# Reordering token loads, pooling chains and norms around a TensorE-bound decoder block

## The chip, the cores and the metric

The kernel runs on one NeuronCore of one Trainium2 chip, as one launch. The metric is the device time of that launch in microseconds (us). The core has five engines that run their own instruction streams in order: TensorE (PE: matmuls, with its weight loads shown apart as PEld), VectorE (DVE), ScalarE (ACT), GpSimd (POOL) and SyncE (SP, which only issues DMAs here). They meet through semaphores. On-chip memory is SBUF (128 partitions) and PSUM, eight banks of 128 x 512 f32 into which TensorE writes.

## The reference, cut to what matters

One hybrid decoder block over 512 tokens of 1024 channels, in f32:

```python
h = rms_norm(x, g_mix_pre)
z = h @ w_in                      # pool 512 | rnn x 1024 | rnn gate 1024 | merge gates 2 x 1024
y_pool = pool_mixer(z_pool) @ w_pool_out   # per group: trailing mean over 2, 4, 8, 16 tokens minus the token, then a 128 x 128 map
y_rnn = rg_lru(z_x, z_g) @ w_rg_out        # causal conv of 4, gates, linear recurrence over tokens, times gelu(z_g)
merged = sigmoid(z_a) * y_pool + sigmoid(z_b) * y_rnn
x = x + rms_norm(merged @ w_o, g_mix_post)
up = rms_norm(x, g_ffn_pre) @ w_up
x = x + rms_norm((gelu(conv3(up_a)) * up_b) @ w_down, g_ffn_post)
ple = rms_norm(p @ w_ple_proj, g_ple_post)
out = x + sigmoid(rms_norm(x, g_ple_gate) @ w_ple_gate) * ple
```

`rms_norm` divides each token by the root of its mean square over all 1024 channels, so each norm needs a sum over a whole token before anything behind it can start.

## The kernel before, in words

**Precision.** TensorE is fed with numbers of fewer bits than f32. Every operand is split into a high half, a rounded copy made by ScalarE (`ACT.copy` into an `fp32r` tile, shown as CAST), and a low half, the difference, made by VectorE (`sub`, line 189). A product then takes three matmuls (`mm3`, lines 219 to 221): high by high, high by low, low by high. So each weight tile needs a DMA (line 426), a ScalarE cast (line 433) and a VectorE subtraction before TensorE can use all of it.

**Weights.** `plan` lists every weight tile in the order of use, and `weight(key, ahead)` prepares up to `ahead` tiles (mostly 4) beyond the one wanted (`prep`). Raw, high and low tiles have six buffers each. Intermediate tiles of 128 x 512 (`slot`) come from a pool of 25 buffers, scratch (`temp`) from one of 5.

**Order of the work.** TensorE's instructions keep the order in which the program is written. Those of the other engines are placed by a planner: it walks through an estimate of the run, and gives each free engine the ready instruction of highest priority. The priority is the place in the program; `tc.high_priority(offset=n)` moves it up by n instructions, and `urgent()` by 700. `behind(ins, name)` fixes the order of two instructions on one engine. Once placed, the order is fixed, and at run time each engine takes its instructions strictly one after another.

**Stages**, in order of time:

1. *Start* (0 to 29 us). `x_t`, the tokens with channels on partitions, arrives in eight pieces of 256 KB; `ht(k)` is the piece times its gain, as high (line 487) and low half (line 488). Four column tiles of the rnn input are computed together from weight pieces rx 0 to rx 3 (line 524). The norm is not applied here: the tokens are loaded once more with tokens on partitions, in two DMAs of 1 MB (`xtok`, line 493), ScalarE squares and sums them (line 507, four instructions), GpSimd raises to the power -0.5 (`rsqrt`, line 455), and VectorE puts the four columns on diagonals (line 515), which TensorE spreads over the partitions with a matrix of ones (`spread_rstd`, line 569) inside the first input tile. The result `rb` is multiplied in when a tile is read from PSUM (`scaled`, line 583). DRAM-to-DRAM sums of weight blocks are issued by GpSimd from behind that `rsqrt` on (line 293).
2. *Input tiles* (29 to 99 us): tiles 0 to 11 of `w_in` (`in_tile`, 24 matmuls each), with conv and the small per-head gate matmuls between them. Then `rnn_decay` (lines 641 to 656, exponentials on ScalarE and scans on VectorE), `rnn_out` and `rnn_split`.
3. *Gate and pool tiles* (99 to about 205 us), in `IN_ORDER`: four gate tiles, then pool tile 0, gate 4, pool 1, gate 5, pool 2, gate 6, pool 3, gate 7, then map 0, gate 8, map 1 and so on. `pool_tile(g)` reads the tile out (`scaled` at offset 300), adds shifted copies log2(window) times (line 712), forms the difference from the token (lines 717 to 719) and splits it (`split`); `pool_map(g)` multiplies it with `pool_w`. `gate_tile` reads out at offset 300 too.
4. *Merge and output projection* (205 to 305 us), with `w_o` by a seven-product scheme on halves. At the end `x2_sum` and `x2_out` form the residual and its norm per token tile (`add_norm`, `rstd_of`), and `h2_tile` transposes and splits it.
5. *Embedding projection* (305 to 317 us): `ple_tile(t)` for four token tiles, all at offset 2100: two PSUM banks of products, each copied to SBUF (lines 769 and 770) and sent to DRAM; `rstd_of(pair)` squares the two banks (line 462). All squares of `rstd_of` are kept in program order by `last_square`.
6. *Up projection* (317 to 366 us for the first part) and *down projection* (to 659 us), again by the seven-product scheme.
7. *End* (650 to 710 us): `x3_norm(t, pair)` makes the second residual and its norm (`add_norm`: line 871 reads the sums, line 462 squares them, line 874 adds; line 1185 applies the gain), `x3_tile(t)` transposes (line 879) and splits it, and the loop from line 1253 on computes the gate in two column halves h with `wpg` weights, four token tiles each. The subtraction for the `wpg` weights of h = 0 has an offset of 1400 (line 434).

Of the kernel before, what the change touches and what calls it, by code (L numbers as in the profile page):

```python
# [14 lines left out]
P = 128  # L15
S = 512
# [65 lines left out]
def block_kernel(  # L82
# [53 lines left out]
    def quad(tag, dt=F32R, place=0):  # L136
        t = big.tile([P, 4 * S + PLACES], dt, tag=tag, name=nm(tag))
        return t[:, place : place + 4 * S].rearrange("p (a c) -> p a c", a=4)
# [23 lines left out]
    def act(o, i, func, after=None, **kw):  # L162

        ins = ACT.activation(o, i, func, **kw)  # L164
        after = after or last_func[0]
        if after is not None:
            behind(ins, after)
        last_func[0] = ins.ins.name
        return ins
# [18 lines left out]
    def sub(o, a, b):  # L188
        V.tensor_tensor(o, a, b, ALU.subtract)  # L189
# [49 lines left out]
    def c1(j):  # L239
        return col[:, j : j + 1]  # L240
# [162 lines left out]
    def prep(key):  # L403
        if key[0] == "up" and key not in parts:
            up_form(*key[1:])
            return
        if key in parts:
            hi, lo = parts_of(D)
            for i, v in enumerate((hi, lo)):
                nc.sync.dma_start(v.bitcast(F32), parts[key][i])  # L410
            if key[0] == "up":
                hi, lo = (v.rearrange("p (j c) -> p j c", j=2) for v in (hi, lo))
            ready[key] = (hi, lo)
            return
        ap = src[key]
        n = 1
        for d in ap.shape[1:]:
            n *= d
        raw = wpool.tile([P, n], F32, tag="raw", name=nm("raw"), bufs=6)
        dst = raw if len(ap.shape) == 2 else raw.rearrange("p (k c) -> p k c", k=ap.shape[1])  # L420
        if key == order[0]:
            nc.sync.dma_start(xraw[0], x_t[0])
            for a, b in FIRST:
                nc.sync.dma_start(raw[:, a:b], ap.rearrange("p k c -> p (k c)")[:, a:b])
        else:
            nc.sync.dma_start(dst, ap)
        hi, lo = parts_of(n)
        if key == order[0]:
            for a, b in FIRST:
                ACT.copy(hi[:, a:b], raw[:, a:b])  # L430
                sub(lo[:, a:b], raw[:, a:b], hi[:, a:b].bitcast(F32))
        else:
            ACT.copy(hi, raw)  # L433
            with tc.high_priority(offset=2 * URGENT if key[0] == "wpg" and key[2] == 0 else 300 if key[0] == "in" and key[1] >= 12 else 0):
                sub(lo, raw, hi.bitcast(F32))
        ready[key] = (hi, lo)

    def weight(key, ahead=AHEAD):
        i = order.index(key)
        while nxt[0] <= min(i + ahead, len(order) - 1):  # L440
            prep(order[nxt[0]])
            nxt[0] += 1
        return ready[key]
# [11 lines left out]
        last_pow[0] = nc.gpsimd.tensor_tensor(y, v, mhalf[:, :n], ALU.pow).ins.name  # L455
        return y

    def rstd_of(halves):
        sums = []
        for hsrc in halves:  # L460
            s = tiny()
            ins = ACT.activation(rb, hsrc, AF.Square, scale=1.0 / 32.0, accum_out=s)  # L462
            if last_square[0] is not None:
                behind(ins, last_square[0])
            last_square[0] = ins.ins.name
            sums.append(s)
        v = tiny()
        V.scalar_tensor_tensor(v, sums[0], EPS, sums[1], ALU.add, ALU.add)  # L468
        return rsqrt(v)
# [7 lines left out]

    xraw = [slot() for _ in range(KD)]
    xtok = []
    for k in range(KD):  # L480
        raw = xraw[k]
        if k == 0:
            weight(("rx", 0), ahead=0)
        else:
            nc.sync.dma_start(raw, x_t[k])
        hi, lo = ht(k)
        ht_done = ACT.activation(hi, raw, AF.Identity, scale=c1(C_GMIX + k)).ins.name
        V.scalar_tensor_tensor(lo, raw, c1(C_GMIX + k), hi.bitcast(F32), ALU.mult, ALU.subtract)
        if k % 2 == 1 and k < 7:
            if k > 1:  # L490
                xt = quad("C", F32)
                a = k // 2 - 1
                nc.sync.dma_start(
                    xt.rearrange("p (a h) c -> p a (h c)", a=2),
                    x[2 * a * P : 2 * (a + 1) * P, :].rearrange("(a p) c -> p a c", p=P),
                )
                xtok.append(xt)
            weight(("rx", k // 2 + 1), ahead=0)


    ssq = tiny(NT)
    for a in range(2):
        xt = xtok[a]
        for b in range(2):
            v = xt[:, 2 * b : 2 * b + 2, :]
            t = 2 * a + b
            ACT.activation(v, v, AF.Square, scale=1.0 / 32.0, accum_out=ssq[:, t : t + 1])
    v4 = tiny(NT)
    V.tensor_scalar(v4, ssq, EPS, None, ALU.add)
    rstd1 = rsqrt(v4, NT)  # L510
# [31 lines left out]
    sp = [const.tile([P, 8], F32, tag=f"sp{i}", name=f"sp{i}") for i in range(7)]  # L542
    mabs, e, f, s, s2, ncol, n2col = sp
    V.scalar_tensor_tensor(mabs, lam, -1.0, lam, ALU.mult, ALU.min)
    act(e, mabs, AF.Exp, after=ht_done)
    V.tensor_scalar(f, e, 1e-37, None, ALU.max)
    act(f, f, AF.Ln)
    sub(f, mabs, f)
# [24 lines left out]
    def in_tile(m):  # L573
        w = weight(("in", m), ahead=AHEAD if m > 6 else AHEAD0)
        ps = bank()
        for k in range(KD):
            mm3(ps, pick(w, k * P, (k + 1) * P), ht(k), k == 0, k == KD - 1)
            if m == 0 and k == 2:
                spread_rstd()
        return ps  # L580

    def scaled(ps, o):
        return V.tensor_tensor(row(o), back(ps), row(rb), ALU.mult)
# [115 lines left out]
    yp, pools = {}, {}  # L699

    def pool_tile(g):
        w = WINDOWS[g]
        ps = in_tile(12 + g)
        u = temp(n=S + PAD)
        V.memset(u[:, :PAD], 0.0)
        with tc.high_priority(offset=300):
            scaled(ps, u[:, PAD:])
        acc, d = u, 1
        while d < w:
            nx = temp(n=S + PAD)  # L710
            o = 2 * d if 2 * d < w else PAD
            V.tensor_tensor(nx[:, o:], acc[:, o:], acc[:, o - d : S + PAD - d], ALU.add)
            acc, d = nx, 2 * d
        u = u[:, PAD:]
        acc = acc[:, PAD:]
        dd = temp()
        V.scalar_tensor_tensor(dd[:, w - 1 :], acc[:, w - 1 :], 1.0 / w, u[:, w - 1 :], ALU.mult, ALU.subtract)
        V.tensor_tensor(acc[:, : w - 1], acc[:, : w - 1], col[:, C_RC : C_RC + w - 1], ALU.mult)
        sub(dd[:, : w - 1], acc[:, : w - 1], u[:, : w - 1])
        hi, lo = slot(F32R), slot(F32R)  # L720
        split(hi, lo, dd)
        pools[g] = hi, lo
# [36 lines left out]
    def ple_tile(t):  # L759
        pair = []  # L760
        for h in range(2):
            w = weight(("wpp", h))
            ps = bank()
            for k in range(2):
                a = pick(pq[k], t * P, (t + 1) * P)
                mm3(ps, a, pick(w, k * S, (k + 1) * S), k == 0, k == 1)
            pair.append(ps)
        outs = [slot(), slot()]
        V.tensor_copy(row(outs[0]), back(pair[0]))
        ACT.copy(row(outs[1]), back(pair[1]))  # L770
        s = rstd_of(pair)
        rp[t] = const.tile([P, 1], F32, tag=f"rp{t}", name=f"rp{t}")
        V.tensor_copy(rp[t], s)
        for h, o in enumerate(outs):
            nc.sync.dma_start(pled[t * P : (t + 1) * P, h * S : (h + 1) * S], o)


    def product(name, lhs, f, banks, start, head=0, tail=0):
# [259 lines left out]

    for t in range(NT):
        with tc.high_priority(offset=3 * URGENT):  # L1040
            ple_tile(t)
        if t == 0:
            x2_out(2)
            x2_sum(3, (oz[1], o5[:, 1]))
        if t == 1:
            h2_tile(1)
            x2_out(3)
    for kind, n in O_AFTER:
        if kind == "tr":
            h2_tile(n)  # L1050
        elif kind == "up":
            up_plain(n, 0)
        else:
            up_product(n, 1)
# [123 lines left out]

    def x3_norm(t, pair):
        res = [x3[t // 2][:, 2 * (t % 2) + h, :] for h in range(2)]  # L1180
        with tc.high_priority(offset=URGENT if t > 1 else 0):
            add_norm(pair, (gq[:, 0, :], gq[:, 1, :]), res)
            for h in range(2):
                x3n[t, h] = nq[t // 2][:, 2 * (t % 2) + h, :]
                V.tensor_tensor(x3n[t, h], res[h], gq[:, 2 + h, :], ALU.mult)
        s3 = rstd_of(res)
        r3[t] = const.tile([P, 1], F32, tag=f"r3{t}", name=f"r3{t}")
        V.tensor_copy(r3[t], s3)

    def x3_tile(t):  # L1190
        xq = hquad(F32R)
        for h in range(2):
            ps = transposed(x3n[t, h])
            x3t[t, h] = xq[:, 2 * h, :], xq[:, 2 * h + 1, :]
            with urgent():
                split(*x3t[t, h], ps)

    gq = quad("C", F32)
# [153 lines left out]
```

## Time and profile before

| | |
|---|---|
| median of 3 runs | 711.7 us (711.26 to 713.67) |
| profiled execution | 712.31 us, span 710.3 us |
| granted TensorE clock | 1.00 |
| TensorE matmul / weight load busy | 699.5 / 637.0 us |
| VectorE, ScalarE, GpSimd busy | 576.6, 441.0, 82.3 us |
| DMA | 172.53 MB, mean 243 GB/s |

The profile is one execution. Its page groups the instructions by line and engine with their busy time, mean length and the idle time before them; the waits name, for each engine, who released it. A timeline row reads: start, length, engine, line, operation, tiles written and read, shapes, count, and in brackets the idle time before it with its releaser. A row of the stretches reads: the stretch, its length, the busy time of TensorE, its weight loads, VectorE, ScalarE and GpSimd, each with its count, then the granted clock, the DMA share and GB/s. Matmuls overlap in the trace, so their lengths add up to more than the time they hold the engine.

### The profile page before, as it was taken

Reading aid. Unit: us, or ns where it says so; the run is one execution under the profiler, and the core shown is the slowest. Engines: PE = TensorE matmul, PEld = TensorE weight load, DVE = VectorE, ACT = ScalarE, POOL = GpSimd, SP = SyncE. Lnnn points to the kernel's source line nnn. Section 1 sums busy time; section 2 is a strip of 40 time slices with the busy share of each in tenths; the row PEclk is TensorE's granted clock in tenths of the full one; section 3 lists DMA queues with packets and bytes.
Section 4 is the critical chain, followed back from the end, with each engine's and each line's share of the span. In section 5 each row is a group of like instructions: output and inputs, shape, how many; then the busy total and the mean of one; then the engine's idle time right before and its main releaser. Section 6 shows DMA issues by size and latency. Waiting matters only on the chain.

```text
span 710.3 us, 11245 instructions
## 1 busy us (share of the span) xinstructions
PE 699.5 (98%) x4281; PEld 637.0 (90%) x4281; DVE 576.6 (81%) x749; ACT 441.0 (62%) x670; POOL 82.3 (12%) x107
## 2 busy tenths in 40 slices
PE   9999999999999999999999999999999999999897
PEld 7888888888888888889999999999999888888786
DVE  3897745999756578776989899899999999789852
ACT  6756789854643245487866677666667766574721
POOL 0311111110000000120013222222200000010100
PEclk9999999999999999999999999999999999999999
DMA  8999787765698999995379999999967677868011
GB/s 318 386 314 279 189 237 162 179 150 189 235 345 271 318 339 357 334 327 187 124 261 267 263 310 251 317 241 337 230 196 232 202 248 229 282 194 290 7 60 59
DMA packets 64933, 172.53 MB, mean 243 GB/s; under 512 B 5808, under 2 KB 6448, under 8 KB 64560
## 3 DMA queue, kind: packets, MB, share of 16 engines
q1 hardware_dynamic: 50336, 129.78, 52.7%
q0 software_dynamic: 14400, 41.95, 25.1%
q8 instruction: 33, 0.54, 0.3%
q14 instruction: 20, 0.16, 0.1%
q10 hardware_dynamic: 144, 0.10, 0.1%
HBM read 155.03 MB, written 58.72 MB: 301 GB/s over the span
## 4 chain that ended last, share of the span: by engine, by line
PE 75%; DVE 12%; ACT 5%; DMA 3%; issue 2%; POOL 1%; SPq 0%; DVEq 0%; POOLq 0%; ACTq 0%
PE ps L219 25%; PE ps L220 25%; PE ps L221 24%; DVE lo L189 3%; ACT m L164 1%; DMA C<-in_x_dram 1%; POOL s L455 1%; DVE m L656 1%; ACT t L164 1%; ACT rb L462 1%; DVE C L189 1%; DMA m<-in_x_t_dram 1%; DVE m L947 1%; PE ps L627 1%; DVE A L1258 1%
## 5 line engine op out<-in xcount | busy, mean ns | idle before, releaser
L189 DVE TENSOR_TENSOR lo<-raw,hi 128x1024 fp32r<-128x1024 f32 (+2 forms) x193 | 224.3, 1184 | 54.3 <-ACT hi L433 40.1
L219 PE MATMUL ps<-A,hi 128*128 128x256 f32 (+1 forms) x608 | 194.5, 320 | 0.0
L220 PE MATMUL ps<-A,hi 128*128 128x256 f32 (+1 forms) x608 | 193.8, 319 | 0.0
L221 PE MATMUL ps<-A,lo 128*128 128x256 f32 (+1 forms) x608 | 193.8, 319 | 0.0
L433 ACT CAST hi<-raw 128x1024 fp32r<-128x1024 f32 (+1 forms) x112 | 112.3, 1010 | 94.4 <-PE ps L220 28.3
L219 PEld LDWEIGHTS ps<-A,hi 128*128 128x128 f32 x608 | 115.9, 191 | 8.4 <-issue 1.3
L221 PEld LDWEIGHTS ps<-A,lo 128*128 128x128 f32 x608 | 116.0, 191 | 6.9
L220 PEld LDWEIGHTS ps<-A,hi 128*128 128x128 f32 x608 | 116.0, 191 | 6.7
L219 PE MATMUL ps<-C,hi 128*128 128x256 f32 (+1 forms) x392 | 114.7, 293 | 1.5 <-ACT rb L462 1.2
L220 PE MATMUL ps<-C,hi 128*128 128x256 f32 (+1 forms) x392 | 114.3, 291 | 0.0
L221 PE MATMUL ps<-C,lo 128*128 128x256 f32 (+1 forms) x392 | 114.3, 291 | 0.0
L193 ACT CAST hi<-raw 128x1024 fp32r<-128x1024 f32 x78 | 80.5, 1050 | 20.5 <-PE ps L220 12.2
L219 PE MATMUL ps<-hi,A 128*128 128x512 f32 x224 | 85.3, 381 | 0.0
L220 PE MATMUL ps<-lo,A 128*128 128x512 f32 x224 | 84.9, 379 | 0.0
L221 PE MATMUL ps<-hi,A 128*128 128x512 f32 x224 | 84.9, 379 | 0.0
L219 PEld LDWEIGHTS ps<-C,hi 128*128 128x128 f32 x392 | 74.7, 190 | 3.9 <-ACT rb L462 1.5
L220 PEld LDWEIGHTS ps<-C,hi 128*128 128x128 f32 x392 | 74.7, 191 | 1.8
L221 PEld LDWEIGHTS ps<-C,lo 128*128 128x128 f32 x392 | 74.7, 191 | 1.7
L455 POOL TENSOR_TENSOR s<-s,mhalf 128x1 f32<-128x1 f32 (+1 forms) x21 | 15.7, 749 | 343.0 <-DVE s L468 323.1
L219 PEld LDWEIGHTS ps<-hi,A 128*128 128x128 f32 x224 | 42.3, 189 | 6.3 <-ACT hi L433 0.3
L221 PEld LDWEIGHTS ps<-hi,A 128*128 128x128 f32 x224 | 42.3, 189 | 6.0
L220 PEld LDWEIGHTS ps<-lo,A 128*128 128x128 f32 x224 | 42.3, 189 | 5.9
(191 smaller groups left out, 1024.7 us busy)
## 6 DMA issues: line engine op xcount, KB each, us to landing
raw<-in_w_up_dram SPq DMA_DIRECT2D x46, 512.0 KB, 8.1
wdsum<-in_w_down_dram POOLq DMA_DIRECT2D x36, 512.0 KB, 9.1
raw<-in_w_in_dram SPq DMA_DIRECT2D x32, 512.0 KB, 7.1
raw<-wdsum SPq DMA_DIRECT2D x24, 512.0 KB, 4.2
raw<-in_w_down_dram SPq DMA_DIRECT2D x18, 512.0 KB, 4.4
wosum<-in_w_o_dram POOLq DMA_DIRECT2D x12, 512.0 KB, 9.7
wdsum<-wdsum POOLq DMA_DIRECT2D x12, 512.0 KB, 8.0
parts<-hi SPq DMA_DIRECT2D x10, 512.0 KB, 5.0
```

Source lines behind the costliest of these rows:

```text
L164: ins = ACT.activation(o, i, func, **kw)
L189: V.tensor_tensor(o, a, b, ALU.subtract)
L193: last_copy[0] = ACT.copy(hi, src)
L219: PE.matmul(o, ah, bh, start=start, stop=False, **kw)
L220: PE.matmul(o, ah, bl, start=False, stop=False, **kw)
L221: PE.matmul(o, al, bh, start=False, stop=stop, **kw)
L433: ACT.copy(hi, raw)
L455: last_pow[0] = nc.gpsimd.tensor_tensor(y, v, mhalf[:, :n], ALU.pow).ins.name
L462: ins = ACT.activation(rb, hsrc, AF.Square, scale=1.0 / 32.0, accum_out=s)
L627: PE.matmul(ps, bd[pr, a, o], turns(b[pr]), start=i == 0, stop=i == 2)
L656: V.tensor_tensor_scan(r, a_t[c], r, 0.0, ALU.mult, ALU.add)
L947: V.scalar_tensor_tensor(h2n[t, h], res[h], r, g_pre[h], ALU.mult, ALU.mult)
```

## The change

Four groups of edits.

- *Start.* The two token loads (`load_tokens`) are issued after rx 3 and after the last `x_t` piece; before, they stood ahead of rx 2 and ahead of rx 3. The square of token tile 0 is placed behind the activation of `x_t` piece 5, the other three behind that of piece 7.
- *Pool chains.* Everything of a pool tile behind its matmuls (`pool_mean`) runs under `urgent()`. The split of the first input tile's weights is urgent as well.
- *Embedding norms.* `ple_tile` only computes, copies and stores; `ple_norm` squares the SBUF copies, is called after the x2 steps of the same token tile, has no offset, and its squares leave the fixed order of squares.
- *Last norms.* `x3_norm` of token tiles 2 and 3 and the splits of their transposes get an offset of 2800; before, 700. The squares for the second norm of every token tile leave the fixed order.

```diff
@@ prep
+        elif key == ("in", 0):
+            with urgent():
+                split(hi, lo, raw)
@@ rstd_of
-    def rstd_of(halves):
+    def rstd_of(halves, in_order=True):
...
-            if last_square[0] is not None:
+            if in_order and last_square[0] is not None:
                 behind(ins, last_square[0])
-            last_square[0] = ins.ins.name
+            if in_order:
+                last_square[0] = ins.ins.name
@@ start
+    ht_done = []
+
+    def load_tokens(a):
+        xt = quad("C", F32)
+        nc.sync.dma_start(
+            xt.rearrange("p (a h) c -> p a (h c)", a=2),
+            x[2 * a * P : 2 * (a + 1) * P, :].rearrange("(a p) c -> p a c", p=P),
+        )
+        xtok.append(xt)
...
-        ht_done = ACT.activation(hi, raw, AF.Identity, scale=c1(C_GMIX + k)).ins.name
+        ht_done.append(ACT.activation(hi, raw, AF.Identity, scale=c1(C_GMIX + k)).ins.name)
...
         if k % 2 == 1 and k < 7:
-            if k > 1:
-                xt = quad("C", F32)
-                a = k // 2 - 1
-                nc.sync.dma_start(
-                    xt.rearrange("p (a h) c -> p a (h c)", a=2),
-                    x[2 * a * P : 2 * (a + 1) * P, :].rearrange("(a p) c -> p a c", p=P),
-                )
-                xtok.append(xt)
             weight(("rx", k // 2 + 1), ahead=0)
+        if k in (5, 7):
+            load_tokens(k // 2 - 2)
...
-            ACT.activation(v, v, AF.Square, scale=1.0 / 32.0, accum_out=ssq[:, t : t + 1])
+            behind(ACT.activation(v, v, AF.Square, scale=1.0 / 32.0, accum_out=ssq[:, t : t + 1]), ht_done[7 if t else 5])
...
-    act(e, mabs, AF.Exp, after=ht_done)
+    act(e, mabs, AF.Exp, after=ht_done[-1])
@@ pool_tile
     def pool_tile(g):
+        ps = in_tile(12 + g)
+        with urgent():
+            pool_mean(g, ps)
+
+    def pool_mean(g, ps):
         w = WINDOWS[g]
-        ps = in_tile(12 + g)
         u = temp(n=S + PAD)
         V.memset(u[:, :PAD], 0.0)
-        with tc.high_priority(offset=300):
-            scaled(ps, u[:, PAD:])
+        scaled(ps, u[:, PAD:])
@@ ple_tile
-        s = rstd_of(pair)
+        for h, o in enumerate(outs):
+            nc.sync.dma_start(pled[t * P : (t + 1) * P, h * S : (h + 1) * S], o)
+        return outs
+
+    def ple_norm(t, outs):
+        s = rstd_of(outs, in_order=False)
         rp[t] = const.tile([P, 1], F32, tag=f"rp{t}", name=f"rp{t}")
         V.tensor_copy(rp[t], s)
-        for h, o in enumerate(outs):
-            nc.sync.dma_start(pled[t * P : (t + 1) * P, h * S : (h + 1) * S], o)
@@ embedding loop
         with tc.high_priority(offset=3 * URGENT):
-            ple_tile(t)
+            outs = ple_tile(t)
         if t == 0:
             x2_out(2)
             x2_sum(3, (oz[1], o5[:, 1]))
         if t == 1:
             h2_tile(1)
             x2_out(3)
+        ple_norm(t, outs)
@@ x3_norm
-        with tc.high_priority(offset=URGENT if t > 1 else 0):
+        with tc.high_priority(offset=4 * URGENT if t > 1 else 0):
             add_norm(pair, (gq[:, 0, :], gq[:, 1, :]), res)
...
-        s3 = rstd_of(res)
+        s3 = rstd_of(res, in_order=False)
@@ x3_tile
-            with urgent():
+            with tc.high_priority(offset=(4 if t > 1 else 1) * URGENT):
                 split(*x3t[t, h], ps)
```

## The prediction

> **What bounds the kernel now.** I read the page first, then the waits of TensorE's weight loads, then the timeline around each of those waits.
>
> ```profile
> span 710.3 us, 11245 instructions
> PE 699.5 (98%) x4281; PEld 637.0 (90%) x4281; DVE 576.6 (81%) x749; ACT 441.0 (62%) x670; POOL 82.3 (12%) x107
> ```
>
> TensorE is busy for 699.5 of 710.3 us, so only the time in which it waits can be won. The waits of its weight loads (engine, line, releaser: us in total, times, longest):
>
> ```profile
> PEld ps L879 <- DVE h L1185: 2.1, 1, 2.1
> ...
> PEld ps L219 <- ACT rb L462: 1.5, 1, 1.5
> PEld ps L220 <- DVE m L189: 1.3, 1, 1.3
> PEld ps L524 <- DVE lo L189: 1.1, 1, 1.1
> PEld ps L524 <- ACT A L487: 1.0, 2, 0.6
> PEld ps L219 <- ACT m L905: 0.6, 1, 0.6
> PEld ps L221 <- DVE h L189: 0.5, 1, 0.5
> ```
>
> Each of the four parts of the change stands at one or two of these rows. Those in its reach: 2.1 + 1.5 + 1.3 + 1.1 + 0.6 (the longer L487 wait) + 0.6 + 0.5 = 7.7 us. That is the most that it can win.
>
> The Trainium skill ("Perfetto Trace Analysis", section "Identifying the Most-Contended Engine") holds matmul busy time a bad measure and takes the busy share of the weight loads. By that share, 90% in the row above, 73 us would be free instead of 7.7, an estimate by that page. The trace does not agree: a load lasts 637.0 / 4281 = 0.15 us on average, while a matmul of 512 columns holds the chain of work for 0.22 us (row below) where nothing waits, so the loads' idle share is no waiting and no end of my range comes from it.
>
> ```profile
> 29.14 0.22 PE ps L220
> ```
>
> **Part A: token loads and squares later.** ScalarE, then the end of the rstd chain that the first input tile needs:
>
> ```profile
> 13.55 1.06 ACT L507 ACTIVATE C<-C 128x1024 f32<-128x1024 f32 x1 [1.62 <-DMA C<-in_x_dram]
> ...
> 16.58 1.33 ACT L487 ACTIVATE A<-m,col 128x512 fp32r<-128x512 f32 x2
> ...
> 18.74 1.06 ACT L507 ACTIVATE C<-C 128x1024 f32<-128x1024 f32 x1 [0.83 <-DMA C<-in_x_dram]
> ...
> 20.84 1.03 ACT L433 CAST hi<-raw 128x1024 fp32r<-128x1024 f32 x1
> ...
> 22.28 0.88 DVE L515 TENSOR_SCALAR t<-ident,s 128x128 f32<-128x128 f32 x4 [1.15 <-POOL s L455]
> ...
> 24.15 1.28 ACT L164 ACT_TABLE_LOAD   x1
> ...
> 30.50 1.07 PEld L569 LDWEIGHTS ps<-t,m 128*128 128x128 f32 x8
> ```
>
> ScalarE waits 1.62 us, then 0.83 us, for the token DMAs, with casts and activations that TensorE wants queued behind. The four squares themselves (about 1.05 us each) stand ahead of the activations at 16.58 and the cast at 20.84. TensorE then waits for the activation (0.6) and the low half of that cast (1.1). Two DMAs of 1 MB move: the first from before rx 2 to after rx 3, the second from before rx 3 to behind x 6 and x 7. No instruction is added. On SP's queue, rx 2, x 4, x 5 and rx 3 each pass 1 MB, and rx 3 passes the second MB too. From 13.55 to 18.74, 2 MB landed (rx 2, x 4, x 5, second token load): 0.39 MB per us. So rx 3 should land at 13.55 - 2.6 + 3.9 = 14.9 against TensorE's need at about 22; the last token load behind 1 MB more, at 18.74 + 2.6 = 21.3. The gain is 0.6 + 1.1 = 1.7; counted at matmul starts, which a load wait shifts by less, about 1.4. I take 1.3; bounds 0 and 1.7.
>
> What is late next: rstd. Two squares after 21.3 end at 23.4 instead of 20.84, so the diagonals end at 23.16 + 2.6 = 25.8. TensorE wants them at 30.50 - 1.4 = 29.1: 3.3 us of cover. The first input tile's cast and low half, now urgent, add 1.03 us to ScalarE's queue there, inside that cover. The POOL queue's DRAM sums, issued behind the rsqrt, start 2.6 us later; that queue idles 137 us later on (row in part C), so nothing waits for them.
>
> The Trainium skill ("ScalarE: Activation LUTs", section "Table sets: the hidden batching unit") says functions come in table sets and only cheap fillers are in each. Squares that fall behind the logarithm's load could need another. With two loads (the page's 2.66 us each, an estimate by it) the cover of 3.3 us would be gone by 2.0. No run here shows squares under that set.
>
> **Part B: pool chains urgent.** VectorE and ScalarE, and the stretch:
>
> ```profile
> 128.60 0.67 DVE L583 TENSOR_TENSOR t<-ps,rb 128x512 f32<-128x512 f32 x1
> ...
> 144.51 2.36 DVE L189 TENSOR_TENSOR lo<-raw,hi 128x1024 fp32r<-128x1024 f32 x2
> ...
> 154.60 0.69 DVE L712 TENSOR_TENSOR t<-t 128x512 f32<-128x512 f32 x1
> ...
> 159.66 0.62 ACT L193 CAST m<-t 128x512 fp32r<-128x512 f32 x1 [6.62 <-DVE t L189]
> ...
> 161.29 0.69 DVE L189 TENSOR_TENSOR m<-t,m 128x512 fp32r<-128x512 f32 x1
> ...
> 161.90 0.69 DVE L583 TENSOR_TENSOR m<-ps,rb 128x512 f32<-128x512 f32 x1
> ...
> 126.00:162.00 36.00, 35.12 (x163) 30.42 (x161) 35.84 (x59) 23.08 (x36) 5.87 (x7) 1.00 0.68 165
> ```
>
> Group 0's sum is read out at 128.60 but its one add waits until 154.60, behind the whole recurrence; its low half ends at 161.98 and TensorE has waited 1.3 us (L220 <- DVE m). With the chain at 700 instead of 300 for its first step and 0 for the rest, group 0 needs a sum, an add, a difference and a low half, 4 x 0.69 plus two corrections of some 0.15: 3.1 us, done near 132. The wait goes: 1.2 taken, bounds 1.3 and a loss below. VectorE is full here (35.84 of 36.00), so the work is traded: groups 0 to 2 (1, 2, 3 adds) take 3.1 + 3.8 + 4.5 = 11.4 us, of which group 0's 3.1 ran there already; up to 8.3 us of recurrence, high/low splits and gates go behind. The splits are wanted only after eight more gate tiles, 40 us on. The nearest cover is that of the weights' low halves: the first of the pair at 144.51 ends by 145.7, and its tile starts two tiles of 24 x 0.22 = 5.3 us before the wait near 161, at 150.5: 4.8 us. These keep an offset of 300 against 0 for the recurrence, so they should stay ahead of it.
>
> **Part C: embedding norms from the copies.** POOL's wait, the squares, and the copies:
>
> ```profile
> 293.38 0.57 POOL L455 TENSOR_TENSOR s<-s,mhalf 128x1 f32<-128x1 f32 x1 [137.34 <-DVE s L468]
> ...
> 317.06 0.60 ACT L462 ACTIVATE rb<-ps 128x512 f32<-128x512 f32 x1
> ...
> 319.41 0.66 ACT L462 ACTIVATE rb<-m 128x512 f32<-128x512 f32 x1
> ...
> 321.76 1.42 DVE L947 SCALAR_TENSOR_TENSOR m<-m,s,m 128x512 f32<-128x512 f32 x2 [0.66 <-POOL s L455]
> ...
> 323.09 1.28 DVE L769 COPY m<-ps 128x512 f32<-128x512 f32 x2
> ...
> 323.89 0.60 ACT L462 ACTIVATE rb<-ps 128x512 f32<-128x512 f32 x1 [2.02 <-DVE m L769]
> ...
> 324.64 0.38 PE L219 MATMUL ps<-C,hi 128*128 128x256 f32 x1 [1.25 <-ACT rb L462]
> ```
>
> TensorE waits at 324.64 for a bank that the embedding's square at 323.89 held after its copy at 323.09. Squares stay eight, at 0.60 and the read of the accumulator; only their source changes (0.66 at 319.41 is one from SBUF), so their price is the same within 0.1 us, and they leave the fixed order of squares and the 2100 priority. Without a change of order a bank is free after the first copy, 323.73, and TensorE starts at about 323.8: 0.8 won. The order moves too: the squares of x2's tile 3 at 319.41 stood behind the embedding's from 317.06, two times 0.8 us, so the copies behind L947 come 1.6 us sooner, at 321.5, and the bank at 322.1, before TensorE's need at 324.64 - 1.5 = 323.1. Then the whole 1.5 goes. The 0.6 before L905 (at 316.89) hangs on the same queue of ScalarE. Sum 2.1; I take 1.6, bounds 0.8 and 2.1. The eight squares now run where ScalarE idles; the price if no idle time is left is 8 x 0.8 = 6.4 us on a queue that idles 41.0 - 31.5 us in the next stretch:
>
> ```profile
> 325.00:366.00 41.00, 41.00 (x363) 40.51 (x362) 33.37 (x47) 31.45 (x58) 1.56 (x3) 1.00 0.45 155
> ```
>
> **Part D: last norms ahead of the low halves.**
>
> ```profile
> 656.26 1.40 DVE L1258 SCALAR_TENSOR_TENSOR A<-A,rp,h 128x512 f32<-128x512 f32 x2
> ...
> 657.58 0.69 DVE L871 TENSOR_TENSOR t<-ps,C 128x512 f32<-128x512 f32 x1
> ...
> 658.38 0.60 ACT L462 ACTIVATE rb<-ps 128x512 f32<-128x512 f32 x1 [6.02 <-DVE t L871]
> ...
> 659.66 0.38 PE L219 MATMUL ps<-hi,h 128*128 128x512 f32 x1
> ...
> 661.78 1.22 DVE L189 TENSOR_TENSOR lo<-raw,hi 128x1024 fp32r<-128x1024 f32 x1
> ...
> 667.32 1.24 DVE L189 TENSOR_TENSOR lo<-raw,hi 128x1024 fp32r<-128x1024 f32 x1
> ...
> 669.08 1.22 DVE L189 TENSOR_TENSOR lo<-raw,hi 128x1024 fp32r<-128x1024 f32 x1
> ...
> 672.41 1.29 DVE L1185 TENSOR_TENSOR h<-C,C 128x512 f32<-128x512 f32 x2
> ```
>
> Token tile 3 is ready to transpose when L1185 ends at 673.7; TensorE has waited 2.1 us for its first half. Its chain has low halves at 667.32 and 669.08 (2 x 1.2 us) in it, which belong to the second column half, wanted three matmul groups of 5.3 us later. Ahead of them the chain ends about 2.4 us sooner, and more, since ScalarE's 6.02 us wait for L871 shortens: L1258 (1.4 us at 656.26) need not come first. The squares of the two residual norms leave the fixed order and the last transposes' copies rise to the same 2800; both only shorten this chain. So 2.1 goes, and most of the 0.5 at L221. But the low half at 661.78 belongs to the first column half and is wanted within a microsecond of its end at 663.0 (it is the fourth of four weights of the group that starts at 659.66, 18 matmuls of 0.22 in); a norm step of two instructions (1.3 us) put ahead of it costs up to 1.3. I take 2.0 of 2.6; bounds 2.6 and 0.8.
>
> **Sum.** 1.3 + 1.2 + 1.6 + 2.0 = 6.1 us. The profiled execution took 712.31 us (span 710.3), 0.6 above the median of 711.7. 712.31 - 6.1 = 706.2; from the median 705.6. I say 706.0.
>
> **Rivals.**
> - *The waits move on a little:* part D pays its 1.3 for the first half's low half and part C gives only its 0.8; 1.3 + 1.2 + 0.8 + 0.8 = 4.1 and 711.7 - 4.1 = 707.6. For it: the cover of under a microsecond at 663.0. Against it: VectorE spends time on L1258, which nothing needs before the last sums.
> - *Token rstd late:* squares and a reload eat the 3.3 us of cover, part A gives nothing: 711.7 - 4.8 = 706.9, or up to 1.4 more with a stall of that size. The table row above (1.28, two loads 2.56) fits inside 3.3 with 0.7 to spare, so this is unlikely alone; by the page's 2.66 it would decide.
> - *Slower: ScalarE blocked by pool splits.* ScalarE waited 6.62 us for group 0's difference at 159.66, and it is in order. If each of the four urgent splits is put as early in its queue and VectorE, full, is as late, it waits 26.5 us from 126 to 162, where it idles 36.0 - 23.1 = 12.9. The weight casts then slip by 13.6, past 4.8 of cover: 8.8 us on TensorE. 711.7 - 4.9 (A, C, D) + 8.8 = 715.6. It decides from about 20 us of such waits. Against it: an urgent chain on VectorE shortens just that wait.
> - *The change does not do what it says:* banks and buffers, not priority, hold the copies and the pool steps; B and C give nothing, 711.7 - 3.3 = 708.4. For it: group 1's sums come only after group 0's low half, as the gate's does (161.90 behind 161.29), which a freed buffer also explains.
>
> **How the numbers follow.** Forecast 0.55, small moves 0.15, rstd late 0.08, banks 0.10, slower 0.12. The range goes from all 7.7 won, 704.0, to the banks' case plus one wait of 2.1, 710.5; that leaves out the slower case and some tails. Within 0.3% is 2.1 us, about what this kernel's runs can tell: faster below 709.6, slower above 713.8. Faster takes the forecast and most of the three milder cases: 0.82; same 0.07, slower 0.11.
>
> **What would show it.** A: the waits at L524 leave the list but for 0.4, and L569's load begins near 29. B: L712's first add near 130, no L220 wait. C: no wait on L462; copies L769 by 322. D: the L879 wait under 0.5 and L1185's last end before 669. Wrong would be a new row of over 2 us in the waits of the weight loads, above all for a low half of a weight between 145 and 165 or at 663.

## The result, and the profile after

The changed kernel takes 719.85 us (median; 719.05 to 720.61) against 712.0 us for the kernel before: a ratio of 1.0107 with an interval of 1.0085 to 1.0128. The change makes the kernel 1.1% slower; the prediction said 706.0 us and a range that ends at 710.5. The profiled execution took 720.01 us.

The first rows of the page of the changed kernel, and the granted TensorE clock in its 40 slices:

```profile
span 718.2 us, 11251 instructions
...
PE 701.1 (98%) x4281; PEld 639.4 (89%) x4281; DVE 577.3 (80%) x749; ACT 441.5 (61%) x670; POOL 82.3 (11%) x107
...
PEclk9999999997999999999999999999999999999999
```

The busy times are those of before to within 0.4%, so most of the 7.9 us are waiting. TensorE's own busy time has grown by 1.6 us, with one thing that was not there before: in the tenth slice (162 to 180 us) the granted clock is below full. The waits of the weight loads in the changed kernel:

```profile
PEld ps L221 <- DVE lo L189: 9.8, 3, 7.0
PEld ps L220 <- DVE lo L189: 3.5, 1, 3.5
```

The rows for `ACT rb`, `DVE m L189` and `DVE h L1185` that the prediction counted are all gone from this list. Four waits for the low half of a weight tile stand in their place. The timeline of TensorE shows the three large ones, and what follows the second:

```profile
29.25 0.48 PE L221 MATMUL ps<-A,lo 128*128 128x512 f32 x1 [1.68 <-DVE lo L189]
...
168.04 0.80 PE L221 MATMUL ps<-m,lo 128*128 128x512 f32 x1 [6.55 <-DVE lo L189]
...
173.35 0.64 PE L220 MATMUL ps<-A,hi 128*128 128x512 f32 x1
173.78 0.53 PE L221 MATMUL ps<-A,lo 128*128 128x512 f32 x1
174.15 0.38 PE L219 MATMUL ps<-A,hi 128*128 128x512 f32 x1
...
674.14 0.48 PE L220 MATMUL ps<-lo,h 128*128 128x512 f32 x1 [3.09 <-DVE lo L189]
```

Both kernels run the same 4281 matmuls in the same order, so the start of each can be subtracted, matmul by matmul. This table is worked out so from the two traces; a step is what the difference changes by at that place.

| start before, us | step, us | what happens there | part |
|---|---|---|---|
| 7 to 9 | -0.34 | first DMAs land a little earlier; the kernels below show +0.1 to -1.3 here | none |
| 17.35, 24.35 | -1.36 | the waits for the activation and for the low half of rx are gone | A |
| 29.20 | +1.75 | low half of the first input tile is late | A |
| 162.03 | -0.98 | the wait for the low half of pool group 0 is gone | B |
| 162.35 | +6.61 | low half of `pool_w` is late | B |
| 162.57 to 165.16 | +3.31 | 13 matmuls at about 0.43 us each instead of 0.215, and a low half of gate 8 (0.3) | B |
| 299 | +0.25 | no wait goes with it | none |
| 316.89, 324.64 | -1.88 | the waits behind the embedding's squares are gone | C |
| 365 | -0.23 | a short wait is gone; it is gone as well in experiments 1 and 9, which have no part C | none |
| 663.76 | +3.25 | low half of the fourth weight of the first column half is late | D |
| 665.5, 673.15, 673.85 | -2.41 | the waits for token tiles 1 and 3 are gone, TensorE being late itself | D |

The sum is +8.0, against 7.9 between the spans (718.2 - 710.3): A +0.39, B +8.94, C -1.88, D +0.84, and -0.32 of no part. The wait that each part was aimed at is gone. Each of A, B and D then pays at a low half that VectorE makes too late.

**A.** ScalarE and then VectorE of the changed kernel at the start:

```profile
19.52 1.04 ACT L515 ACTIVATE C<-C 128x1024 f32<-128x1024 f32 x1
...
20.77 1.28 ACT L164 ACT_TABLE_LOAD   x1
22.06 0.21 ACT L164 ACTIVATE sp<-sp 128x8 f32<-128x8 f32 x1
22.18 1.04 ACT L515 ACTIVATE C<-C 128x1024 f32<-128x1024 f32 x1
...
23.22 1.04 ACT L515 ACTIVATE C<-C 128x1024 f32<-128x1024 f32 x1
```

```profile
20.78 0.17 DVE L554 TENSOR_SCALAR sp<-sp 128x8 f32<-128x8 f32 x1 [0.34 <-ACT sp L164]
...
25.87 0.16 DVE L517 TENSOR_SCALAR s<-s 128x4 f32<-128x4 f32 x1
...
27.18 0.88 DVE L523 TENSOR_SCALAR t<-ident,s 128x128 f32<-128x128 f32 x4 [0.81 <-POOL s L458]
27.98 2.35 DVE L189 TENSOR_TENSOR lo<-raw,hi 128x1024 fp32r<-128x1024 f32 x2
```

The squares now wait for a later DMA, and the planner has put the exponential and the logarithm of the softplus, with its table load, ahead of the last two of the four. VectorE's series behind the logarithm (some twenty instructions of 0.17 us from 22.30 to 26.37) now stands ahead of the step that starts the rstd (L517) and of the diagonals (L523), and the urgent low half stands behind those. The first of its two subtractions ends at 29.2, which is what TensorE waits for at 29.25.

**B.** VectorE of the changed kernel, from group 0's low half to the low half that TensorE waits for:

```profile
134.98 0.69 DVE L189 TENSOR_TENSOR m<-t,m 128x512 fp32r<-128x512 f32 x1
...
161.87 2.48 DVE L189 TENSOR_TENSOR C<-m,C 128x512 fp32r<-128x512 f32 x4
...
166.09 0.68 DVE L189 TENSOR_TENSOR C<-m,C 128x512 fp32r<-128x512 f32 x1
166.69 0.69 DVE L723 TENSOR_TENSOR t<-t 128x524 f32<-128x524 f32 x1
167.30 0.68 DVE L189 TENSOR_TENSOR lo<-raw,hi 128x512 fp32r<-128x512 f32 x1
```

Group 0's low half is ready at 135.67, 25 us ahead of its use. But the low half of `pool_w` (the one of 128 x 512), with which group 0 is multiplied, ends at 167.98. It stands behind the eight splits of the recurrence (`C<-m,C`), which are wanted later and now come later themselves. Its high half was long there; on ScalarE of the same kernel:

```profile
142.26 0.62 ACT L436 CAST hi<-raw 128x512 fp32r<-128x512 f32 x1
```

**C.** The matmul that waited 1.25 us at 324.64 starts at 331.95, without a wait; VectorE's last two copies of the embedding banks come behind it:

```profile
331.95 0.36 PE L219 MATMUL ps<-C,hi 128*128 128x256 f32 x1
```

```profile
332.49 1.28 DVE L780 COPY m<-ps 128x512 f32<-128x512 f32 x2
```

**D.** VectorE of the changed kernel at the end:

```profile
664.30 1.41 DVE L1273 SCALAR_TENSOR_TENSOR A<-A,rp,h 128x512 f32<-128x512 f32 x2 [0.84 <-DMA A<-pled]
665.63 0.68 DVE L885 TENSOR_TENSOR t<-ps,C 128x512 f32<-128x512 f32 x1
...
672.87 1.22 DVE L189 TENSOR_TENSOR lo<-raw,hi 128x1024 fp32r<-128x1024 f32 x1
...
677.00 1.21 DVE L189 TENSOR_TENSOR lo<-raw,hi 128x1024 fp32r<-128x1024 f32 x1
...
680.33 1.29 DVE L1200 TENSOR_TENSOR h<-C,C 128x512 f32<-128x512 f32 x2
```

The norms still begin behind the scalings of the embeddings (L1273), two of which wait for a DMA. The low half at 672.87, which TensorE wants at about 671, now stands behind the norm steps. The two low halves of the second column half, of which 677.00 is the later, stand inside the norm chain as they did before. The last norm ends at 681.6, where it ended at 673.7 before. Of these 7.9 us, 7.1 had come ahead of the tail, so the chain itself became 0.8 us slower. TensorE does not wait for it any more because the new wait at 671 makes TensorE late too.

### The profile page after: what moved, and what is told of

Same layout as the page of the kernel before. It is cut to its first block, busy times and chain, and to the rows that moved or that the text cites. A ratio compares the mean times of both kernels' runs of the same rounds, so it can differ in the third digit from the quotient of the medians.

```text
span 718.2 us, 11251 instructions
## 1 busy us (share of the span) xinstructions
PE 701.1 (98%) x4281; PEld 639.4 (89%) x4281; DVE 577.3 (80%) x749; ACT 441.5 (61%) x670; POOL 82.3 (11%) x107
## 4 chain that ended last, share of the span: by engine, by line
PE 83%; DVE 7%; ACT 4%; DMA 3%; issue 1%; SPq 0%; POOL 0%; DVEq 0%; POOLq 0%
PE ps L219 27%; PE ps L221 27%; PE ps L220 27%; ACT m L164 1%; DMA C<-in_x_dram 1%; ACT t L164 1%; DMA A<-pled 1%; DVE m L664 1%; DVE t L723 1%; PE ps L635 1%; DMA m<-in_x_t_dram 1%; PE ps L893 1%; DVE lo L189 1%; DVE C L189 1%; DVE m L663 1%
## 5 line engine op out<-in xcount | busy, mean ns | idle before, releaser
L189 DVE TENSOR_TENSOR lo<-raw,hi 128x1024 fp32r<-128x1024 f32 (+2 forms) x193 | 224.1, 1182 | 47.6 <-ACT hi L436 29.5
```

## The experiments

**1. The pool chains alone.** The kernel before with only this part of the change:

```diff
     def pool_tile(g):
-        w = WINDOWS[g]
         ps = in_tile(12 + g)
+        with urgent():
+            pool_mean(g, ps)
+
+    def pool_mean(g, ps):
+        w = WINDOWS[g]
...
-        with tc.high_priority(offset=300):
-            scaled(ps, u[:, PAD:])
+        scaled(ps, u[:, PAD:])
```

> The kernel before with the pool chains made urgent and nothing else changed. Theory (the low half of pool_w, which has no priority of its own, falls behind the delayed splits of the recurrence; the wait is so long that TensorE's clock drops): the whole loss of that stage comes with this part alone, +8.9 us by the shift of the matmuls between the two traces, so 721; one wait of 6 to 7 us for a low half at the first pool map and a granted clock near 0.5 for some 5 us behind it. Rival (the loss needs the other parts, which bring TensorE there 1 us earlier): below 716.

Measured: 720.54 us, ratio 1.0118 (1.0097 to 1.0139). The waits of its weight loads begin with

```profile
PEld ps L221 <- DVE lo L189: 7.8, 2, 7.0
```

and its steps at this place are -1.09, +6.64 and then about +3.6. Part B alone costs what the whole change costs, so the other parts are not needed for it, and the rival falls.

**2. The change without the pool chains.** The edit of experiment 1 taken back in the changed kernel.

> The changed kernel with the pool chains back at their old priorities. Theory: the start nets 0, the embedding stage gives 1.9, the end costs 0.8, so 712.0 - 1.1 = 710.9, no slow clock, and the old wait of 1 us at the first pool map back. Rival (the parts hang together through the planner, and the loss moves elsewhere): above 715.

Measured: 711.64 us, ratio 0.9992 (0.998 to 1.0005), 0.7 above what was expected; the rival falls. The three other parts together gain nothing that can be told from no change. In the trace C's -1.9 remains, while A (1.30 won, 1.77 lost at the first input tile) and D (2.41 won, 2.37 lost) give their gains back. That trace ends 2.0 us earlier than the one of before, which the median does not show. The profiled execution (710.06 us) is the shortest of ten: its mean granted clock is 1.00, that of eight others 0.997, as in the profile of experiment 3, where a stretch of half clock stands behind the stall at the end. Where it stands in these eight no trace shows.

**3. The low half of `pool_w` put in its place.** The changed kernel with one offset:

```diff
-... else 300 if key[0] == "in" and key[1] >= 12 else 0):
+... else 300 if key == "pool_w" or key[0] == "in" and key[1] >= 12 else 0):
```

> The changed kernel with one number more: the subtraction for pool_w gets the offset of 300 that the input weights from tile 12 on have. Theory: its wait of 6.6 us, the 0.5 us wait behind it and the slow clock go together, 9.9 us: 710. Rival (VectorE is simply too full with the pool chains ahead, whichever instruction comes last): the wait moves to another low half or to a gate's bank, and more than 4 us of it stay: 714 or more.

Measured: 710.87 us, ratio 0.9984 (0.9969 to 0.9999): 9 us below the changed kernel, by one number, as expected; the rival falls. VectorE of this kernel makes the low half 21 us earlier than in the changed one:

```profile
146.34 0.67 DVE L189 TENSOR_TENSOR lo<-raw,hi 128x512 fp32r<-128x512 f32 x1
```

Part B then keeps its -0.98, with no wait and no slow stretch behind it. So the loss of part B is this one subtraction in the wrong place, and the slow clock there comes with it. A and D of this kernel still pay at their own low halves (1.6 at 29 us; 3.7 at 663 us and 1.4 of slow clock behind it).

**4. Three orders mended.** Experiment 3's kernel, with the exponential behind the last token square and the low half of the fourth gate weight raised above the norms:

```diff
-... offset=2 * URGENT if key[0] == "wpg" and key[2] == 0 else ...
+... offset=(6 if key[1] == 3 else 2) * URGENT if key[0] == "wpg" and key[2] == 0 else ...
...
+            sq_done = ACT.activation(v, v, AF.Square, ...)
-            behind(ACT.activation(v, v, AF.Square, ...), ht_done[7 if t else 5])
+            behind(sq_done, ht_done[7 if t else 5])
...
-    act(e, mabs, AF.Exp, after=ht_done[-1])
+    act(e, mabs, AF.Exp, after=sq_done.ins.name)
```

> As the one before, and two more: the subtraction for the last weight of the first column half at 4200 instead of 1400, and the softplus exponential placed behind the last token square instead of behind the last x_t activation. Theory (each new wait is one low half that lost its place): 3.2 us less at the end, 1.7 us less at the first input tile: 705. Rival for the end (the cast on ScalarE, which waits behind a square, is what is late): 708 to 709 and the wait named ACT. Rival for the start (the first tile's cast lands late whatever VectorE does): 1.5 us of wait stay there.

Measured: 707.5 us, ratio 0.9941 (0.9921 to 0.9961), faster than the kernel before but short of the 705 expected. In the trace A keeps its gain, B and C too (-5.3 by 366 us), and the wait for the low half of the fourth gate weight is gone. One wait of over 2 us is left, and it stands in the tail:

```profile
PEld ps L221 <- DVE h L189: 2.2, 1, 2.2
```

VectorE of the same kernel there:

```profile
651.45 1.42 DVE L1274 SCALAR_TENSOR_TENSOR A<-A,rp,h 128x512 f32<-128x512 f32 x2 [0.31 <-DMA A<-pled]
652.78 0.69 DVE L886 TENSOR_TENSOR t<-ps,C 128x512 f32<-128x512 f32 x1
...
660.56 0.68 DVE L886 TENSOR_TENSOR t<-sum,C 128x512 f32<-128x512 f32 x1
661.16 1.28 DVE L189 TENSOR_TENSOR h<-ps,h 128x512 fp32r<-128x512 f32 x2
```

Now the low half of token tile 1 is late, behind the first step (L886) of the last norm. Two causes were open: its place, or the scalings (L1274), which stand ahead of everything.

**5. The scalings last, and the low halves of token tile 1 raised.** Experiment 4's kernel with

```diff
-                V.tensor_tensor(x3n[t, h], res[h], gq[:, 2 + h, :], ALU.mult)
+                last_x3[0] = V.tensor_tensor(x3n[t, h], res[h], gq[:, 2 + h, :], ALU.mult).ins.name
...
-            with tc.high_priority(offset=(4 if t > 1 else 1) * URGENT):
+            with tc.high_priority(offset=(4 if t else 1) * URGENT):
...
-            V.scalar_tensor_tensor(v, v, rp[t], gp[:, h, :], ALU.mult, ALU.mult)
+            behind(V.scalar_tensor_tensor(v, v, rp[t], gp[:, h, :], ALU.mult, ALU.mult), last_x3[0])
```

> This is the kernel of the three mended orders (707.5 us) with two more moves in its tail on VectorE: the eight scalings of the embeddings stand behind the last token tile's norm, and the low halves of the second token tile stand ahead of that norm. Theory (the norms of the last token tiles are held by the order of work on VectorE, which has no idle time from 644 to 663 us): the 1.7 us wait for the low half of the second token tile goes, and the last norms come some 2 us earlier, so that the remaining waits of the tail go as well: 707.5 - 1.7 - 1 to 1.5 = about 704.5 us (704 to 705.8). Rival (the norms are held by TensorE's banks or by ScalarE's squares, and VectorE's order only decides which low half is late): 706.5 or more, with a new wait of over 1.5 us in the tail.

Measured: 704.3 us (704.14 to 704.53), ratio 0.9893 (0.9878 to 0.9908), as expected and the fastest of all. The longest wait of the weight loads that is left is one of 1.1 us in the first microseconds, which the kernel before has too. VectorE of this kernel is ahead of the sums and waits for TensorE, where it was behind before:

```profile
649.82 0.69 DVE L886 TENSOR_TENSOR t<-ps,C 128x512 f32<-128x512 f32 x1 [1.25 <-PE ps L221]
...
664.32 1.28 DVE L1202 TENSOR_TENSOR h<-C,C 128x512 f32<-128x512 f32 x2
```

The last norm ends at 665.6 instead of 673.7 in the kernel before; 5.3 of these 8.1 us were won ahead of the tail.

**6. The same two moves, one at a time.** The second line of experiment 5's edit alone, then the first and third alone, each on experiment 4's kernel.

> The kernel of the three mended orders (707.5 us), with one move: the low halves of the second token tile stand ahead of the last token tile's two gain products on VectorE; the scalings stay where they are. It parts the two moves of the 704.3 us kernel. If its gain is all in the late low half (theory 1), the time is near 704.5 us. If the scalings count, because they hold the first of the last two norms by some 3 us (theory 2), the 1.7 us wait for the low half goes but the wait for that norm's last tile comes back behind it: 706.5 to 707.7 us.

> The kernel of the three mended orders (707.5 us), with the other move alone: the eight scalings behind the last token tile's norm. By theory 2 (the scalings hold the norm) VectorE has come some 5 us of work earlier when the low halves of the second token tile are wanted, so that they are no longer late although they stand behind the gain products: 704 to 705 us. By theory 1 (only the place of those low halves counts) the wait of about 1.7 us stays: 706 us or more.

Measured: 707.1 us (ratio 0.993, 0.991 to 0.995) with the low halves raised, 704.99 us (0.9896, 0.9879 to 0.9913) with the scalings last. With the low halves raised the wait only moves to the last token tile:

```profile
PEld ps L894 <- DVE h L1201: 2.1, 1, 2.1
```

This is the wait that the kernel before had, at its old length (the trace is of an execution of 709.15 us, with 3.4 us of half clock behind that wait). With the scalings last both waits are gone. The scalings, eight times 0.66 us that nothing needs before the last sums, are what held the norms. No run has the scalings last without part D, so whether the raised priorities are needed beside that order is open.

**7. The mended kernel without part D.** Experiment 4's kernel with the priorities and the order of squares of the tail as before.

> The kernel of the three mended orders (707.5 us), with the part on the norms of the last token tiles undone (priorities and chain of squares as before). Theory (that part gains nothing and costs the waits of low halves that it makes late): the tail is as in the kernel before, so that the gains of the other parts stand alone: 711.8 - 5.3 = 706.5 us (706 to 707.2), below the kernel with the part. Rival (the part gains something behind the wait that it makes): 707.5 or more.

Measured: 707.64 us (ratio 0.9934, 0.9918 to 0.995), no different from the 707.5 with the part. The trace agrees with the theory (end -5.23 us, and the 2.1 us wait of before back in the tail, in the same row as in experiment 6), but the median is 1.1 us above what the theory gave and falls on the rival's side. The two medians cannot be told apart: part D, even with its one late low half mended, shows no gain by itself.

**8. The exponential alone.** The changed kernel with the last two edits of experiment 4's diff only.

> The changed kernel (719.85 us) with one edit: the exponential of the softplus stands on ScalarE behind the squares of the last token tile, so that VectorE's series behind it comes behind the first low halves, as it did before. Theory (the series on VectorE took back the gain of the earlier token squares): the wait of 1.75 us at the first tile's third product goes and the 1.7 us won until there is kept: 719.85 - 1.75 = 718.1 us (717.6 to 718.6). Rival (the wait comes from GpSimd's rstd, which the order on VectorE does not move): 719.4 or more.

Measured: 718.24 us (ratio 1.0084, 1.0067 to 1.0101), 1.6 below the changed kernel as expected. ScalarE of this kernel does all four squares before the table load, VectorE does the diagonals at once and the series later, and TensorE does not wait at the first input tile:

```profile
24.18 0.87 DVE L524 TENSOR_SCALAR t<-ident,s 128x128 f32<-128x128 f32 x4 [1.15 <-POOL s L458]
24.97 2.35 DVE L189 TENSOR_TENSOR lo<-raw,hi 128x1024 fp32r<-128x1024 f32 x2
27.24 0.16 DVE L555 TENSOR_SCALAR sp<-sp 128x8 f32<-128x8 f32 x1
```

The wait of GpSimd is longer here than in the changed kernel (1.15 against 0.81), so the rival that blames it falls. The diagonals come 3.0 us earlier than in the changed kernel, and not by VectorE's order alone. The squares end 1.5 us earlier (22.83 against 24.35), of which 0.5 is an earlier start; the step behind them (L517, here L518), which the series held for 1.5 us, follows them at once.

**9. The last norms alone.** The kernel before with only part D (the diff of `x3_norm`, `x3_tile` and `rstd_of` in the change, without `ple_norm`).

> The kernel before with the part on the norms of the last token tiles alone. Theory (that part moves one weight's low half behind two adds of a norm, and with it loses about 3.2 us at 664 us against 2.4 us that come back behind it): 711.8 + 0.8 = 712.6 us (712.0 to 713.5), with a wait of 2.5 to 4 us of the weight loads for a low half of a weight near 663 us. Rival (the low half is late in the changed kernel only because of the other parts): 711 or less, without that wait.

Measured: 713.19 us (711.04 to 715.31), ratio 1.0013 (0.9998 to 1.0028): by time alone it cannot be told from no change. The times fall in two groups: five executions with a mean granted clock of 0.999 or 1.00 took 711.0 to 712.5 us, seven with 0.997 or 0.995 took 713.1 to 715.3. That points to the half clock behind its stall as the main cost of this part by itself. The trace, of one of the seven, shows the mechanism without the other parts, so the rival falls: a wait of

```profile
PEld ps L220 <- DVE lo L189: 3.1, 1, 3.1
```

and behind it, in the stretches of this kernel (the granted clock is the third number from the end), a TensorE at half clock:

```profile
664.00:666.50 2.50, 0.00 (x0) 0.00 (x0) 2.50 (x5) 2.39 (x6) 0.00 (x0) 1.00 0.00 0
...
668.00:669.00 1.00, 1.00 (x4) 0.80 (x3) 0.93 (x1) 0.46 (x2) 1.00 (x1) 0.50 0.00 0
```

## Why the prediction was wrong, step by step

The forecast was -6.1 us and the measured change about +8. The step that turned it is part B's: -1.2 was forecast, +8.9 came, for a low half whose cover was not looked up. The waits of A, B and C went as forecast (1.36, 0.98 and 1.88 against 1.3, 1.2 and 1.6); the gain of D did not come at all.

**The bound.** Right: the waits of the weight loads were the whole stake. The 704.3 us of experiment 5 is 7.7 us below the 711.96 of before beside it, which is what the prediction gave as the most to be won. That it is the same number is in part luck: in the trace 0.6 of it comes from the first DMAs and 0.2 from the step at 365, which belong to no part.

**A, -1.3.** The gain was there: 1.36. The step that failed is "inside that cover": the cover was counted for the rstd on ScalarE's queue alone, from the squares to TensorE's ones-matmuls. Indeed no wait for the rstd appears. What was not listed is what else the planner would put in the gap that it opens for the squares, and what then stands behind it on VectorE. Experiment 8 shows it to be the softplus: its logarithm's table load on ScalarE, ahead of the last two squares, and its series on VectorE. Together they cost 1.75. No run takes the urgent split of the first input tile's weights apart from the moved loads. The rival of a reloaded table did not occur either: the last two squares ran from 22.18, right behind the logarithm, with no second load. The Trainium skill ("ScalarE: Activation LUTs", section "Table sets: the hidden batching unit") says that tables are loaded as named sets, and does not name the square among the functions that are in every set. The trace of the change has one load, at 20.77, and the squares at 22.18 and 23.22 follow without another, so the set loaded for that logarithm serves them too.

**B, -1.2.** The wait of group 0 went, with 0.98. The step that failed is "the nearest cover is that of the weights' low halves ... these keep an offset of 300 against 0 for the recurrence". That holds for the input tiles of the gates. The low half of `pool_w` has an offset of 0 and a place in the program behind the recurrence's splits, so it was pushed back by the urgent chains on a VectorE that is full, and it is wanted at the same moment as group 0. In the kernel before it was made at this place, in a row that the prediction did not look up:

```profile
155.21 0.69 DVE L189 TENSOR_TENSOR lo<-raw,hi 128x512 fp32r<-128x512 f32 x1
```

TensorE used it at 162.35, so its cover was 6.5 us, against 8.3 us of work that the prediction itself reckoned to be moved behind. In the changed kernel it ends 12.1 us later, with first steps of group 3 (L723 at 166.69 among them) ahead of it too, which the 8.3 did not count. Experiment 3 shows that the place of this one subtraction is all of it. The second omission is the price: a wait of 6.6 us costs about 2.8 more in half-clock matmuls. The slower rival came near the cost (8.8 against 8.9) by luck and at the wrong engine: ScalarE had the cast of `pool_w` done by 142.9, VectorE was late, and a third of the cost is the half clock, which the rival did not have.

**C, -1.6.** Right in size: 1.88, between the bounds of 0.8 and 2.1, and 1.9 in every kernel here that has the part; experiments 1 and 9, without it, keep the wait of 1.5. So the rival in which it gives nothing falls. The path is only half as predicted. TensorE no longer waits for a square to give a bank free. But the copies of VectorE, which were to come 1.6 us sooner ("copies L769 by 322"), come at 332.49, which is 2.1 us later as TensorE's work counts (332.49 less its shift of 7.3 there is 325.2, against 323.09), and behind the matmul at 331.95. Which copy gave that matmul its bank is not shown.

**D, -2.0.** Two steps failed. "Ahead of them the chain ends about 2.4 us sooner" supposed that the offset of 2800 puts the norm ahead of the two low halves of the second column half. They stayed in the chain, and it ended 0.8 us later instead; the -2.41 of the table is no gain of the norm but the other side of the new wait. An offset only ranks work that is ready, and the norm was not: its first step stood behind the scalings, which the prediction saw ("need not come first") but counted as if the priority would move them. Experiment 6 shows that moving them wins 2.5, with the two low halves still in the chain. The other is the price "up to 1.3" of a norm step ahead of the low half at 661.78: several steps came ahead of it, and it was 3.25.

**The chances.** The prediction's own sign of being wrong, a row of over 2 us for a low half of a weight between 145 and 165 or at 663, came true at both places (162.35 and 663.76 by the times of before). The doubt was on paper, with 0.11 on it, and it was priced as a ScalarE matter.

## What to carry to other kernels

Before a chain is made urgent on a full engine, list every instruction of that engine that TensorE needs between the old and the new place of the chain, with its own priority and its own slack; here the one with the lowest priority paid, and it was the other operand of the very matmul that was to be sped up. If a priority does not move a chain, look at what stands ahead of it on its engine: work that is ready early and needed late (eight scalings) held the last norms, and ordering that work last won more than raising the chain. A stall on TensorE can cost some 40% more in the clock behind it (2.8 behind 6.6 us), or nothing (behind 3.09 us).

## What the runs showed of the hardware

After some idle stretches of TensorE the granted clock fell to 0.5, and each matmul of 512 columns took 0.43 us instead of 0.215. It stayed there for 10.24 us in the changed kernel (163.84 to 174.08, six of them with matmuls) and for 3.41 us in experiments 3, 9 and the run with the low halves raised. The changed kernel around its longest wait, in stretches:

```profile
161.00:168.00 7.00, 0.49 (x3) 0.09 (x1) 7.00 (x13) 3.26 (x5) 0.00 (x0) 0.70 0.00 0
168.00:170.00 2.00, 1.87 (x4) 1.06 (x5) 2.00 (x3) 0.00 (x0) 0.00 (x0) 0.50 0.47 127
...
172.00:174.00 2.00, 2.00 (x6) 1.56 (x5) 2.00 (x5) 0.61 (x1) 0.00 (x0) 0.50 0.83 296
...
674.00:675.00 1.00, 0.86 (x4) 0.78 (x5) 1.00 (x3) 0.98 (x3) 0.00 (x0) 1.00 0.00 0
```

The length of the stretch alone does not decide it. It followed idle times of 6.55 us, of 3.53 us in experiment 3, of 2.66 us in experiment 9, and once of 1.74 us (the run with the low halves raised); it did not follow 3.09 us in the changed kernel (last row above), nor 2.20 us in the profile of experiment 2, nor 1.74 us in the kernel before. In the changed kernel it came 2.3 us into the idle time that began at 161.49 (the 0.70 of the first row gives the same start).

The clock records of the traces show a grid: each change lies a whole number of steps of 3.413 us behind the one before it (46, 3 and 159 steps in the changed kernel). Worked out from these records and the matmul times, half clock followed every step of the running kernel in which TensorE was idle for 2.29 us or more, and no step with 1.77 us or less. Between these it followed 1.78 us but not 1.93, and matmul ends are modelled, so the exact rule stays open. The 3.09 us of the changed kernel fell into two steps, as 1.37 and 1.72 us.

The rule of the Trainium skill ("TensorE: Matmul & The Clock Gate", section "What's actually happening") is that the clock is halved after an idle window of about 3.4 us, and that the windows run free of the program. The half clock and the free-running steps agree with the runs; that 2.66 us was enough does not fit a window that must be idle throughout.
